# Rotary keys of a head pair: one whole split of the transposed bank, doubled tiles by GpSimd, and a low product over 64 rows

## The chip, the cores and the metric

The kernel runs on one core of one Trainium2 chip. The core's engines work side by side, each through its own queue of instructions: TensorE (PE in the profile, with PEld for its weight loads), VectorE (DVE), ScalarE (ACT), GpSimd (POOL) and SyncE (SP, which here issues most DMAs). Matmul results land in PSUM, in banks of 128 partitions by 512 fp32 values; everything else lies in SBUF, 128 partitions wide. GpSimd has no operation on PSUM in this kernel. The metric is device time of one execution in microseconds.

## What is computed

A trunk of two layers over 512 tokens of width 2048: a gated pooling mixer, then latent attention with 16 heads. The part that matters here is the score of a query with a key. A head's query and key have 128 plain channels and 64 rotary ones; the rotary key is the same for all heads but for the norm of the head's key.

```python
k = qk_norm_rope(concatenate([k_nope, k_rope]), k_norm_g, cos, sin)   # 128 + 64 channels
q = qk_norm_rope(q, q_norm_g, cos, sin)
for i in range(S // QBLOCK):                       # 4 blocks of 128 queries
    s = einsum('bqhd,bkhd->bhqk', q[:, q0:k_end], k[:, :k_end]) * scale
    s = where(mask, s, -1e30)                      # block-causal, chunks of 64
    p = softmax(s)
    outs.append(einsum('bhqk,bkhd->bqhd', p, v[:, :k_end]))
```

All of it is fp32.

## The kernel before

Every fp32 product is made of three products of a shorter type (float32r): a value x is split into a high part, x rounded to that type, and a low part, x minus the high part, and hi·hi + hi·lo + lo·hi are summed in PSUM. The split is a ScalarE copy (high) and a VectorE subtraction (low). `split` (line 153) does both, with the helper's line 154 in the profile for both of them.

The attention stage handles the 16 heads as eight head pairs. For each pair, key, value and query projections run in small pieces (lines 662 to 664 and 685 to 687 are their matmuls), and between them the scores, softmax and outputs of the pair before. Which piece comes when is written out by hand: a list of pieces with estimated times, and a main loop over 64 score units (pair, head, block of 128 queries) that fills the time between softmax steps with pieces. TensorE keeps exactly the order of the program; the instructions of the other engines are put in order by a planner.

Steps that the change and the prediction touch:

- `krot_unit` (line 713): GpSimd scales the rotary key by each head's norm into one tile, `krs`, two heads of 64 channels side by side.
- `tr_unit(hg, 2)` (lines 749 to 767): four TensorE transposes (line 754) bring `krs` to a PSUM bank, p: rows 0 to 63 are head 0's rotary channels, rows 64 to 127 head 1's, 512 tokens long. Then, for each head: GpSimd clears rows 64 to 127 of the low tile `kl` (762), ScalarE copies the head's 64 rows to the high tile `kh` twice, to its upper and lower half (763, 764), and VectorE writes the low part into the upper half of `kl` (765). From pair 1 on this unit stands in the main loop beside the sixth score unit of the pair before.
- `tr_unit(hg, 5)`: the same for the rotary query, whose high part goes to rows 0 to 63 and low part to rows 64 to 127 of one tile per head (781, 782). The other values of u transpose the plain channels of keys (0, 1) and queries (3, 4), all through line 776.
- `score_unit` (line 794): five matmuls (810) into one bank: three of the plain channels, one of the query tile (high over low) with `kh` (high twice), which gives hi·hi + lo·hi in a single product over 128 rows, and one of the same query tile with `kl` (low over zeros), which gives hi·lo, also over 128 rows.
- After it come the row maximum (813, 815), the exponential on ScalarE (823), the scaling on VectorE (829, 830), and the transposes of the probabilities (`pt_unit`, 838).

All these transposes share two PSUM banks of the tag "tr", which are used in turn: the next but one set of transposes waits until the set before has been read out. SBUF tiles of the tag "b" come from a pool of 32 buffers, also in turn.

Of the kernel before, what the change touches and what calls it, by code (L numbers as in the profile page):

```python
# [8 lines left out]
F32R = mybir.dt.float32r  # L9
I32 = mybir.dt.int32  # L10
AF = mybir.ActivationFunctionType
ALU = mybir.AluOpType
AX = mybir.AxisListType

P = 128
S = 512
# [31 lines left out]
def trunk_kernel(  # L48
# [17 lines left out]
    V, A, G, T = nc.vector, nc.scalar, nc.gpsimd, nc.tensor  # L66

    const = ctx.enter_context(tc.tile_pool(name="const", bufs=1))
    rpool = ctx.enter_context(tc.tile_pool(name="rpool", bufs=2))
# [3 lines left out]
    def xt(shape=(P, S), dt=F32):  # L73
        return xpool.tile(list(shape), dt, tag="x", name="xt")
# [4 lines left out]
    def at(dt=F32R, shape=(P, S)):  # L79
        return apool.tile(list(shape), dt, tag="a", name="at")  # L80

    def bt(shape=(P, S), dt=F32R):
        return bpool.tile(list(shape), dt, tag="b", name="bt")
# [10 lines left out]
    def sc():  # L94
        return ps.tile([P, S], F32, tag="sc", name="sc", bufs=2)

    def tr():
        return ps.tile([P, S], F32, tag="tr", name="tr", bufs=2)

    def f(ap):  # L100
        return ap.bitcast(F32)
# [51 lines left out]
    def split(src, hi, lo):  # L153
        return A.copy(hi, src), V.tensor_tensor(lo, src, f(hi), ALU.subtract)  # L154
# [112 lines left out]
    with ExitStack() as c1:  # L267
# [106 lines left out]
        with ExitStack() as c2:  # L374
            hp = c2.enter_context(tc.tile_pool(name="hp", bufs=2, **tile_))
            for j in range(NJ):
# [5 lines left out]
                hi = w7.tile([P, 4, 2, P], F32R, tag="hi", name="hi")  # L382
                lo = w7.tile([P, 4, 2, P], F32R, tag="lo", name="lo")
# [42 lines left out]
        for n, pair in enumerate((*range(18, 32), *range(16))):  # L426
# [7 lines left out]
            if n == 9:  # L434
                V.tensor_tensor(sq[0], sq[0], sq[1], ALU.add)
                p = ps7[0].tile([P, 2, H], F32, tag="k3", name="k3").rearrange("p h t -> p (h t)")
# [79 lines left out]
    for k in range(KD):  # L516
        hi, lo = at(), at()
        gsplit(xr[k], C_GKV + k, hi, lo)
        xkv.append((hi, lo))
        hi, lo = bt(), bt()  # L520
# [67 lines left out]
    kr = krb[:, 0:256].rearrange("p (t d) -> p t d", t=4)  # L588
# [48 lines left out]
    def small(n=8, tag="sm", bufs=6):  # L637
        return spool.tile([P, n], F32, tag=tag, name=tag, bufs=bufs)
# [107 lines left out]
    def tr_unit(hg, u):  # L746

        d = st[hg]
        if u == 2:

            d["kr"] = []
            p = tr()
            for t in range(4):
                T.transpose(p[:, t * P:(t + 1) * P], d["krs"][:, t * P:(t + 1) * P], ident)
            for h in range(2):
                src = p[h * 64:h * 64 + 64, :]
                if hg:
                    kh = bt()
                else:
                    kh = xt(dt=F32R) if h else rpool.tile([P, S], F32R, tag="r", name="kr0")  # L760
                kl = bt()
                G.memset(f(kl[64:128, :]), 0.0)
                A.copy(kh[0:64, :], src)
                A.copy(kh[64:128, :], src)
                V.tensor_tensor(kl[0:64, :], src, f(kh[0:64, :]), ALU.subtract)
                d["kr"].append((kh, kl))
            return
        p = tr()
        for t in range(4):
            if u < 2:  # L770
                src = d["kraw"][t // 2][:, t % 2, u * P:(u + 1) * P]
            elif u < 5:
                src = d["qraw"][t][:, u - 3, 0:128]
            else:
                src = d["qrot"][:, t * P:(t + 1) * P]
            T.transpose(p[:, t * P:(t + 1) * P], src, ident)  # L776
        if u == 5:
            q0, q1 = bt(), bt()
            for h, q in enumerate((q0, q1)):
                src = p[h * 64:h * 64 + 64, :]  # L780
                A.copy(q[0:64, :], src)
                V.tensor_tensor(q[64:128, :], src, f(q[0:64, :]), ALU.subtract)
            d["qr"] = (q0, q1)
            return
        ft = at if hg == 0 and u in (0, 3) else bt
        hi, lo = ft(), ft()
        if u in (3, 4):
            A.activation(hi, p, AF.Copy, scale=gqk)
            V.scalar_tensor_tensor(lo, p, gqk, f(hi), ALU.mult, ALU.subtract)
        else:  # L790
            split(p, hi, lo)
        d[("T", u)] = (hi, lo)

    def score_unit(hg, h, i):
        d = st[hg]
        n = (i + 1) * P
        if i == 2:

            gt = d[("G", h)] = bt(dt=F32)
            nc.sync.dma_start(gt, gates[2 * hg + h])  # L800
        s = sc()
        kh, kl = d[("T", h)]
        krh, krl = d["kr"][h]
        qh, ql_ = d[("T", 3 + h)]
        qr = d["qr"][h]
        qs = slice(i * P, (i + 1) * P)
        ops = [(qh[:, qs], kh[:, 0:n]), (qh[:, qs], kl[:, 0:n]), (ql_[:, qs], kh[:, 0:n]),
               (qr[:, qs], krh[:, 0:n]), (qr[:, qs], krl[:, 0:n])]
        for j, (l, r) in enumerate(ops):
            T.matmul(s[:, 0:n], l, r, start=(j == 0), stop=(j == 4))  # L810
        V.memset(s[0:64, n - 64:n], -1e30)
        nm = small(1, "nm", 4)
        V.tensor_reduce(nm, s[:, 0:n], AX.X, ALU.max)
        rq = d["rq"][:, 2 * i + h:2 * i + h + 1]
        V.scalar_tensor_tensor(nm, nm, -1.0, rq, ALU.mult, ALU.mult)
        d[("P", h, i)] = s, nm, rq
# [207 lines left out]
    for m, (key, w) in enumerate(keys):  # L1024
        n = last[keys[m - 4][0]] if m >= 4 else -1
# [48 lines left out]
    for m in range(len(seq) + 2):  # L1074
        now = seq[m] if m < len(seq) else None
        if now:
            hg, h, i = now
# [105 lines left out]
```

## Time and profile before

| | us |
|---|---|
| median of 3 runs | 1920.48 (1920.28 to 1922.47) |
| the profiled execution | 1920.45 |
| its span in the profile | 1918.7 |
| TensorE busy in the span | 1902.5 (99%) |
| VectorE busy | 1299.6 (68%) |
| ScalarE busy | 829.2 (43%) |
| GpSimd busy | 286.9 (15%) |

The profile shows one execution. A timeline row reads: start, duration, engine, line, operation, output tile <- input tiles, shape, how many in a row; in brackets how long the engine stood idle before it and what the profile takes for the releaser. In a row of a group, what follows the bar is the busy time, the mean of one in ns, and the idle time before. In a row of a line's instructions, three numbers in ns are the shortest, the median and the longest. Ends of matmuls are modelled, and one matmul overlaps the next, so how fast TensorE goes is read from the distance of their starts, not from their durations. Granted clock of TensorE was full (0.999) over the whole span.

The stage of the projection layers lasts until about 1450 us; the eight head pairs until about 1765 us, some 35.2 us each in the middle; the output projection takes the rest.

### The profile page before, as it was taken

The page shows a single profiled execution, that of the slowest core. Times are in us where ns is not written, and L with a number is a line of the kernel's source. Part 1 is how long each engine was busy: PE and PEld are TensorE (multiplying, and loading weights), DVE is VectorE, ACT ScalarE, POOL GpSimd, SP SyncE. Part 2 cuts the span into 40 slices and gives each one's busy share as a digit, 9 for nine tenths or more (in the row PEclk, how much of TensorE's full clock was granted, in tenths as well). Part 3 has the DMA queues.
Part 4 walks back from the last instruction along what each step waited for, and adds up shares of the span by engine and source line. Part 5 has one row for each costly group of instructions (what it writes and reads, how often), then busy time and mean ns, then how long its engine had stood idle before and what let it go on. Part 6 is the DMA issues. An engine that isn't in the chain of part 4 may idle for free.

```text
span 1918.7 us, 30196 instructions
## 1 busy us (share of the span) xinstructions
PE 1902.5 (99%) x11084; PEld 1688.6 (88%) x11084; DVE 1299.6 (68%) x2282; ACT 829.2 (43%) x1555; POOL 286.9 (15%) x436
## 2 busy tenths in 40 slices
PE   8999999999999999999999999999999999999999
PEld 7999999999999988888888888888888888988887
DVE  8677796897766786586695576574335888887332
ACT  8444433333333442332432354233236787775221
POOL 0433343333232100000000000000001332320000
PEclk9999999999999999999999999999999999999999
DMA  6555444444454556334334344334443232244642
GB/s 191 158 162 159 150 132 133 123 129 138 145 151 131 167 172 199 115 119 152 118 124 137 105 150 132 93 99 121 116 120 95 82 96 77 74 128 143 200 117 87
DMA packets 177077, 251.24 MB, mean 131 GB/s; under 512 B 15776, under 2 KB 96800, under 8 KB 176928
## 3 DMA queue, kind: packets, MB, share of 16 engines
q1 hardware_dynamic: 176640, 249.10, 42.3%
q8 instruction: 87, 1.43, 0.3%
q14 instruction: 62, 0.51, 0.1%
q10 hardware_dynamic: 288, 0.20, 0.0%
HBM read 216.21 MB, written 33.03 MB: 130 GB/s over the span
## 4 chain that ended last, share of the span: by engine, by line
PE 93%; DVE 3%; DMA 2%; ACT 1%; issue 1%; POOL 0%; SPq 0%; DVEq 0%; POOLq 0%; ACTq 0%
PE mm L149 16%; PE mm L151 16%; PE mm L150 16%; PE k L346 10%; PE k L344 9%; PE k L342 9%; PE k L339 3%; PE sc L810 2%; PE mm L662 1%; PE mm L664 1%; PE mm L663 1%; PE mm L685 1%; PE mm L686 1%; PE mm L687 1%; PE tr L838 1%; PE tr L776 1%
## 5 line engine op out<-in xcount | busy, mean ns | idle before, releaser
L131 ACT CAST whi<-raw 128x512 fp32r<-128x512 f32 (+2 forms) x424 | 256.2, 607 | 539.4 <-PE mm L150 439.9
L132 DVE TENSOR_TENSOR wlo<-raw,whi 128x512 fp32r<-128x512 f32 (+2 forms) x424 | 283.8, 670 | 242.7 <-ACT whi L131 239.7
L346 PE MATMUL k<-xc,lo 128*128 128x256 f32 x1680 | 417.4, 283 | 0.8 <-DVE lo L320 0.8
L344 PE MATMUL k<-xc,hi 128*128 128x256 f32 x1440 | 397.5, 283 | 0.0
L342 PE MATMUL k<-xc,hi 128*128 128x256 f32 x1440 | 396.8, 282 | 0.0
L151 PE MATMUL mm<-bt,wlo 128*128 128x512 f32 x944 | 368.0, 390 | 0.0
L149 PE MATMUL mm<-bt,whi 128*128 128x512 f32 x944 | 367.7, 390 | 0.0
L150 PE MATMUL mm<-bt,whi 128*128 128x512 f32 x944 | 367.0, 389 | 0.0
L320 DVE TENSOR_TENSOR lo<-raw,hi 128x1792 fp32r<-128x1792 f32 x120 | 249.3, 2078 | 131.7 <-ACT hi L319 131.5
L319 ACT CAST hi<-raw 128x1792 fp32r<-128x1792 f32 x120 | 203.2, 1693 | 285.7 <-PE k L346 172.5
L346 PEld LDWEIGHTS k<-xc,lo 128*128 128x128 f32 x1680 | 302.7, 190 | 8.3 <-DVE lo L320 2.0
L342 PEld LDWEIGHTS k<-xc,hi 128*128 128x128 f32 x1440 | 273.3, 190 | 5.0
L344 PEld LDWEIGHTS k<-xc,hi 128*128 128x128 f32 x1440 | 273.7, 190 | 0.0
L151 PEld LDWEIGHTS mm<-bt,wlo 128*128 128x128 f32 x944 | 177.1, 188 | 37.3 <-issue 0.5
L149 PEld LDWEIGHTS mm<-bt,whi 128*128 128x128 f32 x944 | 177.3, 188 | 36.9 <-ACT whi L131 0.2
L150 PEld LDWEIGHTS mm<-bt,whi 128*128 128x128 f32 x944 | 177.2, 188 | 36.7
L150 PE MATMUL mm<-at,whi 128*128 128x512 f32 x432 | 168.6, 390 | 0.3 <-DVE at L154 0.3
L149 PE MATMUL mm<-at,whi 128*128 128x512 f32 x432 | 168.8, 391 | 0.0
L151 PE MATMUL mm<-at,wlo 128*128 128x512 f32 x432 | 168.2, 389 | 0.0
L315 POOL TENSOR_TENSOR raw<-raw 128x256 f32<-128x256 f32 x120 | 97.5, 812 | 428.3 <-DVE raw L313 410.1
L316 POOL TENSOR_TENSOR raw<-raw 128x256 f32<-128x256 f32 x120 | 110.0, 917 | 9.2
L150 PEld LDWEIGHTS mm<-at,whi 128*128 128x128 f32 x432 | 81.1, 188 | 17.3 <-DVE at L154 0.6
(1137 smaller groups left out, 2714.2 us busy)
## 6 DMA issues: line engine op xcount, KB each, us to landing
raw<-awin SPq DMA_DIRECT2D x240, 256.0 KB, 3.4
raw<-awo SPq DMA_DIRECT2D x128, 256.0 KB, 2.7
raw<-bwin SPq DMA_DIRECT2D x80, 256.0 KB, 2.9
raw<-awg SPq DMA_DIRECT2D x64, 256.0 KB, 2.7
scr<-e SPq DMA_DIRECT2D x56, 256.0 KB, 2.7
raw<-bwo SPq DMA_DIRECT2D x56, 256.0 KB, 2.9
raw<-wkvb SPq DMA_DIRECT2D x32, 256.0 KB, 3.1
raw<-wqb SPq DMA_DIRECT2D x32, 192.0 KB, 2.4
```

Of the source, the lines that this page charges most:

```text
L131: wsplits[:] = (A.copy(hi[:, :n], raw[:, :n]).ins, V.tensor_tensor(lo[:, :n], raw[:, :n], f(hi[:, :n]), ALU.subtract).ins)
L132: V.tensor_tensor(lo[:, :n], raw[:, :n], f(hi[:, :n]), ALU.subtract).ins)
L149: T.matmul(dst, wh, xh, start=first, stop=False)
L150: T.matmul(dst, wh, xl, start=False, stop=False)
L151: T.matmul(dst, wl, xh, start=False, stop=last)
L315: G.tensor_tensor(c[:, :, 6, :], c[:, :, 4, :], c[:, :, 2, :], ALU.add)
L316: G.tensor_tensor(c[:, :, 7, :], c[:, :, 6, :], c[:, :, 3, :], ALU.add)
L319: A.copy(hi, c[:, :, 1:8, :])
L320: V.tensor_tensor(lo, c[:, :, 1:8, :], f(hi), ALU.subtract)
L342: T.matmul(dst, hi[:, j % 2, wi, :], xh[j][:, xi, :], start=first, stop=False, skip_group_check=True)
L344: T.matmul(dst, hi[:, j % 2, wi, :], xl[j][:, xi, :], start=False, stop=False, skip_group_check=True)
L346: T.matmul(dst, lo[:, j % 2, wi, :], xh[j][:, xi, :], start=False, stop=last, skip_group_check=True)
```

## The change

In `tr_unit(hg, 2)` the bank is split whole: one ScalarE copy of all 128 rows to `k0` and one VectorE subtraction of all 128 rows to a single low tile `kl`. `k0` then holds head 0's high rows above and head 1's below. GpSimd makes the doubled tiles from it: it copies `k0`'s lower half to both halves of `k1`, and then `k0`'s upper half over its lower half. The two clearings of low tiles are gone, and one low tile is needed instead of two.

The low tile now holds head 0's low rows in partitions 0 to 63 and head 1's in 64 to 127, with nothing to mask the other head. So the fifth matmul of a score unit contracts only the head's own 64 partitions, and the query's high part has to lie in the same partitions: for head 1 the query tile is turned over, low part above, high part below. The fourth matmul, over 128 rows with the doubled high tile, is indifferent to that.

```diff
@@ tr_unit, u == 2
-            d["kr"] = []
             p = tr()
             for t in range(4):
                 T.transpose(p[:, t * P:(t + 1) * P], d["krs"][:, t * P:(t + 1) * P], ident)
-            for h in range(2):
-                src = p[h * 64:h * 64 + 64, :]
-                if hg:
-                    kh = bt()
-                else:
-                    kh = xt(dt=F32R) if h else rpool.tile([P, S], F32R, tag="r", name="kr0")
-                kl = bt()
-                G.memset(f(kl[64:128, :]), 0.0)
-                A.copy(kh[0:64, :], src)
-                A.copy(kh[64:128, :], src)
-                V.tensor_tensor(kl[0:64, :], src, f(kh[0:64, :]), ALU.subtract)
-                d["kr"].append((kh, kl))
+            if hg:
+                k0, k1 = bt(), bt()
+            else:
+                k0, k1 = rpool.tile([P, S], F32R, tag="r", name="kr0"), xt(dt=F32R)
+            kl = bt()
+            split(p, k0, kl)
+            for half in (slice(0, 64), slice(64, 128)):
+                G.tensor_copy(k1[half, :], k0[64:128, :])
+            G.tensor_copy(k0[64:128, :], k0[0:64, :])
+            d["kr"] = (k0, kl[0:64, :]), (k1, kl[64:128, :])
             return
@@ tr_unit, u == 5
             for h, q in enumerate((q0, q1)):
                 src = p[h * 64:h * 64 + 64, :]
-                A.copy(q[0:64, :], src)
-                V.tensor_tensor(q[64:128, :], src, f(q[0:64, :]), ALU.subtract)
-            d["qr"] = (q0, q1)
+                hi, lo = q[h * 64:h * 64 + 64, :], q[64 - h * 64:128 - h * 64, :]
+                A.copy(hi, src)
+                V.tensor_tensor(lo, src, f(hi), ALU.subtract)
+            d["qr"] = (q0, q0[0:64, :]), (q1, q1[64:128, :])
             return
@@ score_unit
-        qr = d["qr"][h]
+        qr, qrh = d["qr"][h]
...
-               (qr[:, qs], krh[:, 0:n]), (qr[:, qs], krl[:, 0:n])]
+               (qr[:, qs], krh[:, 0:n]), (qrh[:, qs], krl[:, 0:n])]
```

## The prediction

> **What bounds the kernel now.** I read the top of the page first, then the chain that ended last, then the timeline of one head pair.
>
> ```profile
> PE 93%; DVE 3%; DMA 2%; ACT 1%; issue 1%; POOL 0%; SPq 0%; DVEq 0%; POOLq 0%; ACTq 0%
> ```
>
> TensorE carries 93% of the chain, so time can only be won where it stands still, and lost where it is given more work or a new wait. The change touches only the attention stage, where the scores run from 1480 to 1763 us, eight head pairs of about 35 us each. In that stage I looked for matmuls that start later than the one before them allows. A 512-column matmul is followed by the next after 0.227 us when nothing is late (the rows for this stand below, with the cost of small matmuls). In every middle pair one place is late. The timelines of ScalarE, VectorE and TensorE in one of them, just after the four transposes of the rotary k (start, duration, engine, line, in us):
>
> ```profile
> 1541.72 0.58 ACT L763 CAST bt<-tr 64x512 fp32r<-64x512 f32 x1 [0.86 <-PE tr L754]
> 1542.31 0.58 ACT L764 CAST bt<-tr 64x512 fp32r<-64x512 f32 x1
> 1542.92 0.56 ACT L823 ACTIVATE tt__15373<-sc,nm,qy 128x256 f32<-128x256 f32 x1
> ```
> ```profile
> 1542.92 0.68 DVE L765 TENSOR_TENSOR bt<-tr,bt 64x512 fp32r<-64x512 f32 x1 [0.56 <-ACT bt L764]
> ...
> 1544.31 0.34 DVE L830 TENSOR_SCALAR tt__15373<-tt__15373,sm 128x256 f32<-128x256 f32 x1
> ```
> ```profile
> 1544.27 0.40 PE L664 MATMUL mm<-wlo,at 128*128 128x512 f32 x1
> 1544.80 0.41 PE L838 MATMUL tr<-cs,tt__15373 128*128 128x128 f32 x2
> ```
>
> The exponential of a score row (L823) stands on ScalarE behind the two copies of the split, its scaling (L830) on VectorE behind the split's subtraction and a reduction that the engine takes in between, and the transposes of that row (L838) start only when the scaling is done: 1544.80 instead of 1544.27 + 0.23 = 1544.50. **0.30 us** lost. The next pairs repeat it, five in all; the last of them loses 1685.69 - 1685.15 - 0.23 = 0.31:
>
> ```profile
> 1685.15 0.40 PE L664 MATMUL mm<-wlo,at 128*128 128x512 f32 x1
> 1685.69 0.41 PE L838 MATMUL tr<-cs,tt__17629 128*128 128x128 f32 x2
> 1685.85 0.48 PE L662 MATMUL mm<-whi,at 128*128 128x512 f32 x1
> ```
>
> In the pair that is split first inside the loop, and in the last, the loss is larger and sits one step later:
>
> ```profile
> 1509.01 0.39 PE L664 MATMUL mm<-wlo,at 128*128 128x512 f32 x1
> ...
> 1509.67 0.69 DVE L765 TENSOR_TENSOR bt<-tr,bt 64x512 fp32r<-64x512 f32 x1
> ...
> 1510.51 0.63 PE L776 MATMUL tr<-cs,qt 128*128 128x128 f32 x4 [1.11 <-DVE qy L168]
> ```
> ```profile
> 1722.71 0.38 PE L838 MATMUL tr<-cs,tt__18213 128*128 128x128 f32 x2
> ...
> 1724.65 0.63 PE L776 MATMUL tr<-cs,qt 128*128 128x128 f32 x4 [1.56 <-DVE qy L168]
> ```
>
> The transposes of the q side (L776) need one of the two transposed banks, and the one whose turn it is still holds rotary k until the second head's subtraction (L765) ends, at 1510.36. The profile puts this wait down to a small VectorE operation that ends just after (line 168), on which these transposes do not depend; the same engine's subtraction before it is the one they need. Late by 1510.51 - 1509.01 - 0.23 = **1.27 us**, and in the last pair by 1724.65 - 1722.71 - 0.16 = **1.78 us** (0.16 for two transposes, as between 1685.69 and 1685.85). Together the rotary split costs TensorE 1.27 + 5 x 0.30 + 1.78 = **4.6 us**, which is the ceiling of what the change can win there.
>
> **The change part by part.**
>
> *The split of the bank.* Removed per pair: four ScalarE copies of 64 rows (0.58 each) and two subtractions (0.69 each); added: one copy and one subtraction of 128 rows, for which the same forms stand in the trace:
>
> ```profile
> L154 ACT CAST bt<-tr x15: 587/608/621, 1484.8 to 1736.5; 128x512 fp32r<-128x512 f32 x15
> L154 DVE TENSOR_TENSOR bt<-tr,bt x15: 665/691/693, 1485.5 to 1737.3; 128x512 fp32r<-128x512 f32 x15
> ```
>
> ScalarE gives back 4 x 0.58 - 0.61 = 1.7 us a pair, VectorE 0.69. The bank is free 0.61 + 0.69 after the copy starts instead of 3.8 us after. In the steady pair: copy 1541.72 to 1542.33, exponential until about 1543.0, scaling over by about 1543.7, before the 1544.50 at which its transposes are due, and still in time if one other VectorE operation of 0.6 us comes first. In the pair at 1509 the bank would be free near 1508.4 (needed 1509.24), in the last near 1722.5 (needed 1722.85), where the copy waits behind other ScalarE work until 1720.68 in the old order. What is late next there is nothing that I can see, so I count 4.2 of the 4.6 us as won and leave 0.4 for the last pair's thin margin and the contention below.
>
> *GpSimd's three copies.* No such copy is in the trace. Nearest rows:
>
> ```profile
> L762 POOL MEMSET bt<- 64x512 f32 x16 | 8.3, 521 | 0.9
> ```
> ```profile
> L720 POOL TENSOR_TENSOR tt__15238<-krr,sy 128x256 f32<-128x256 f32 x2 | 2.1, 1060 | 1.7 <-DVE nm L815 1.7
> ```
> ```profile
> 1551.57 0.67 PE L810 MATMUL sc<-bt 128*128 128x128 f32 x5
> ```
> ```profile
> 1528.44 0.50 POOL L741 TENSOR_TENSOR tt__15132<-qt,qcos 128x128 f32<-128x128 f32 x1 [22.09 <-ACT qt L691]
> ```
> ```profile
> L763 ACT CAST kr<-tr x1: 581/581/581, 1474.4 to 1474.4; 64x512 fp32r<-64x512 f32 x1
> ```
> ```profile
> 1481.11 0.27 PE L810 MATMUL sc<-kr,bt 128*128 128x128 f32 x1
> ```
>
> Lower end 0.52 each (same shape, nothing read), upper end 2 x 1.06 = 2.1 (two inputs, twice the columns); I take 0.7, nearer to the same shape. Three make 2.1 us, with ends 1.6 and 6.4 (rounded from 3 x 2.12); two memsets (1.04) go. They begin when ScalarE's copy is done, 1542.4, and the next pair's first score needs them at 1551.57: even the upper end leaves 2.8 us, so TensorE does not see them. Nothing is queued behind them: GpSimd's next work is 22 us away, as the row of its first operation in a pair shows. If that cover were gone, the price would be the copies themselves, 2 us a pair. In pair 0 the split's copy starts at 1474.4 and a score first reads the tile at 1481.1; 6.1 us are left for the copies, which covers 2.1 us nearly three times over, and the upper end but for 0.3. No DMA is added or moved, and no load is passed; the pool that held four tiles a pair holds three, so buffers come free no later.
>
> Against VectorE they are not free:
>
> ```profile
> 1503.92 0.86 DVE L132 TENSOR_TENSOR wlo<-raw,whi 128x512 fp32r<-128x512 f32 x1
> ```
> ```profile
> 1504.19 0.77 POOL L742 TENSOR_TENSOR tt__14569<-qt,qsin 128x64 f32<-128x64 f32 x1
> ```
>
> With a GpSimd operation beside it the subtraction took 0.86, where one of this shape otherwise takes 0.67 to 0.69 (L154 above). So each copy may hold VectorE by 0.2 to its own 0.7 us, right when the scaling is due. The slack of 0.8 us found above takes one such hold; two or three would bring back part of the 0.30.
>
> The Trainium skill, "SBUF — State Buffer", section "SBUF: two separate sides", calls the pair of ports that GpSimd and VectorE share an exclusive lock: whichever starts first keeps it for the whole instruction and the other blocks. By that rule a VectorE operation with two SBUF inputs would lose the full copy, so it speaks for the rival in which less of the stall goes; the rows above show a delay of 0.19 us beside a GpSimd time of 0.77, less than a full hold.
>
> *The low product over 64 rows.* Each of the 64 score units (8 pairs, 2 heads, 4 row blocks) now has a fifth matmul that contracts 64 rows, between matmuls over 128. The columns that stream are the same, so I give the matmul the same length. (The q side's four operations per pair keep their shapes and only change rows: nothing.) What is unknown is the price of going from the full array to half its rows and back. No such matmul is in the trace; the nearest in kind is the rotary latent, which switches between 128 and 64 columns of weights at every step:
>
> ```profile
> 1226.35 0.39 PE L579 MATMUL mm<-at,whi 128*128 128x512 f32 x1
> ...
> 1229.34 0.40 PE L579 MATMUL mm<-at,whi 128*128 128x512 f32 x1
> ```
> ```profile
> 1218.65 0.39 PE L151 MATMUL mm<-at,wlo 128*128 128x512 f32 x1
> ...
> 1221.82 0.39 PE L150 MATMUL mm<-at,whi 128*128 128x512 f32 x1
> ```
>
> 13 steps in 2.99 us are 0.230 each, against 14 in 3.17, 0.226 each, without switching: 4 ns a switch. The other end is the change from fp32 transposes to the split products:
>
> ```profile
> 1611.88 0.48 PE L662 MATMUL mm<-whi,at 128*128 128x512 f32 x1
> 1612.20 0.39 PE L663 MATMUL mm<-whi,at 128*128 128x512 f32 x1
> ```
>
> 0.32 us to the next instead of 0.23: 0.09 a switch. With two switches a unit and 64 units the ends are 128 x 0.004 = 0.5 us and 128 x 0.09 = 11.5 us. For a gain I find no row: half the weights' width saves none of the 0.23 above, so the lower end stays at 0.5. I take 0.5, the row that is a switch of the array's shape.
>
> **Sum.** -4.2 + 0.5 = -3.7 us on the profiled execution's 1920.45 us (the span below and 1.75 around it): 1916.75.
>
> ```profile
> span 1918.7 us, 30196 instructions
> ```
>
> The median of the runs shown is 1920.48, so the forecast is **1916.8 us**, 0.19% faster.
>
> **Rivals.**
>
> *Half the rows is a costly switch (slower).* Each of the 128 switches makes TensorE wait until the matmul before is through and its weights cannot be loaded ahead. Price 0.06 to 0.18 us a unit: 3.8 to 11.5 us, so 1920 to 1928. It cancels the gain at 4.2 / 64 = 0.066 us a unit and makes the kernel slower by 0.2% (3.8 us) from 0.126. Against it: 4 ns for the switch in columns. For it: rows and columns of the array need not behave alike, and 0.09 exists for another switch.
>
> The Trainium skill, "TensorEngine Tiling (Array Packing)", section "Tiling Modes", says that changing the tiling mode drains TensorE. By that rule this rival would hold; at the one change of mode that this trace has (128 to 64 columns) no drain of any size shows, 4 ns.
>
> *Less of the stall goes.* GpSimd's copies hold VectorE, or the new order on ScalarE and VectorE puts the reduction first: the five 0.30 stay, only 1.27 + 1.78 go. 1920.45 - 3.1 + 0.5 = 1917.9, up to 1920 if one large stall stays too. This is also the case in which the change does not do what it says.
>
> *More goes.* 1.7 us of ScalarE and 0.7 of VectorE a pair come free; one more place in the last pair where TensorE stands idle, 0.66, goes with it:
>
> ```profile
> 1703.99 0.41 PE L838 MATMUL tr<-cs,tt__17902 128*128 128x128 f32 x2 [0.66 <-DVE sc L811]
> ```
>
> 1920.45 - 4.6 - 0.7 + 0.5 = 1915.7, down to 1914 with other places of the kind.
>
> *A worse order.* ScalarE, VectorE and the load queue are ordered anew by a planner; a wait like that of the last pair (1.8 us) appears in one or several pairs: 1921 to 1926.
>
> **How the numbers follow.** Forecast 0.46, costly switch 0.22, less 0.14, more 0.12, worse order 0.06. A measurement of this kernel can tell about 0.2% from no change: under 1916.6 is faster, over 1924.3 slower. Faster: 0.25 of the forecast (its own range, 1915.5 to 1918.5, straddles the line) and all of "more": 0.37. Slower: 0.12 of the costly switch and 0.05 of the worse order: 0.17. Same: the rest of these cases and all of "less", 0.46. The range 1914.0 to 1923.5 leaves out the dear half of the costly switch, the worst orders, and little below.
>
> **What would show it.** Right: L776 follows without idle time in the pairs near 1510 and 1724; L838 comes 0.23 us after L664 in the middle pairs; each pair's period falls from 35.2 to 34.9; matmuls over 64 rows follow one another within 0.23 us at 512 columns; GpSimd's copies last 0.5 to 2.1 us and no matmul waits for them. Wrong: gaps of 0.06 us or more before and behind the matmul over 64 rows in all 64 units (costly switch); scalings on VectorE that stretch or start late beside a GpSimd copy (less); new idle time of TensorE at another line (order).

## The result, and the profile after

The changed kernel takes 1937.66 us (median of six runs, 1936.43 to 1938.31) against 1922.01 for the kernel before, measured beside it (six runs, 1920.28 to 1923.46): a ratio of 1.0082, with a 95% interval of 1.0069 to 1.0095. It is slower by about 16 us. The forecast was 1916.8, and its range ended at 1923.5. The execution that was profiled took 1937.78 us, against 1920.45 before. The top of the page of the kernel after:

```profile
span 1935.9 us, 30161 instructions
...
PE 1923.5 (99%) x11084; PEld 1691.5 (87%) x11084; DVE 1295.4 (67%) x2274; ACT 817.1 (42%) x1531; POOL 292.6 (15%) x444
...
PE 95%; DVE 2%; DMA 1%; ACT 1%; issue 1%; SPq 0%; POOL 0%; DVEq 0%; ACTq 0%; POOLq 0%
```

ScalarE and VectorE have less to do (829.2 and 1299.6 us before), TensorE as many instructions as before and 21 us more of "busy" time. Its share of the chain rose from 93 to 95%. So the loss is not, in the main, a new wait for another engine: TensorE itself has become slower, and the window of the attention stage says where (columns: stretch, its length, then busy time and count of PE, PEld, DVE, ACT, POOL; clock, DMA share, GB/s). First the kernel before, then the one after:

```profile
1456.00:1765.00 309.00, 304.04 (x1817) 271.63 (x1816) 257.93 (x839) 228.30 (x720) 76.08 (x160) 1.00 0.32 96
```
```profile
1456.00:1782.00 326.00, 324.74 (x1817) 274.58 (x1816) 253.73 (x830) 215.64 (x695) 83.66 (x168) 1.00 0.30 90
```

The same 1817 matmuls of the attention stage take 326.0 us instead of 309.0, at full clock: 17.0 us of the 17.2 by which the span has grown (1935.9 - 1918.7). Next, one score unit of 384 columns and the three matmuls behind it, in TensorE's timeline; before, then after. Ends are modelled, so the starts are what counts:

```profile
1612.66 1.05 PE L810 MATMUL sc<-bt 128*128 128x384 f32 x5
1613.55 0.39 PE L662 MATMUL mm<-whi,at 128*128 128x512 f32 x1
1613.78 0.40 PE L663 MATMUL mm<-whi,at 128*128 128x512 f32 x1
1614.02 0.40 PE L664 MATMUL mm<-wlo,at 128*128 128x512 f32 x1
```
```profile
1546.13 1.25 PE L808 MATMUL sc<-bt 128*128 128x384 f32 x5
1547.31 0.51 PE L662 MATMUL mm<-whi,at 128*128 128x512 f32 x1
1547.65 0.40 PE L663 MATMUL mm<-whi,at 128*128 128x512 f32 x1
1547.89 0.40 PE L664 MATMUL mm<-wlo,at 128*128 128x512 f32 x1
...
1548.58 0.39 PE L664 MATMUL mm<-wlo,at 128*128 128x512 f32 x1
1548.81 0.38 PE L836 MATMUL tr<-cs,tt__15365 128*128 128x128 f32 x2
```

From the first score matmul to the third matmul behind the unit it was 1.36 us and is 1.76: **0.40 us more in a unit**, with no wait shown. The last two rows are the place that lost 0.30 in every middle pair before: the transposes now follow L664 after 0.23, so that stall has gone, as forecast. The timeline of the weight loads (PEld) for the same two units shows what differs, before and then after:

```profile
1612.43 0.96 PEld L810 LDWEIGHTS sc<-bt 128*128 128x128 f32 x5
1613.38 0.19 PEld L662 LDWEIGHTS mm<-whi,at 128*128 128x128 f32 x1
```
```profile
1545.90 0.78 PEld L808 LDWEIGHTS sc<-bt 128*128 128x128 f32 x4
1546.94 0.18 PEld L808 LDWEIGHTS sc<-bt 64*128 64x128 f32 x1 [0.26 <-issue]
1547.31 0.19 PEld L662 LDWEIGHTS mm<-whi,at 128*128 128x128 f32 x1 [0.19 <-issue]
```

Before, the weights of the matmul behind a unit (L662) were loaded from 1613.38, 0.17 us ahead of its start at 1613.55. After, the load of the 64 rows waits 0.26 us, and the load behind it, which goes back to 128 rows, starts at 1547.31, the moment at which its matmul starts. Neither is loaded ahead any longer.

Taken over all 64 units, from the starts of the matmuls in both traces (medians in us, 16 units of each size; the order of the matmuls is the same in both):

| columns | before: fifth matmul behind the fourth, next, next but one | after | more in the unit, with one matmul further |
|---|---|---|---|
| 128 | 0.111, 0.112, 0.226 | 0.205, 0.254, 0.284 | 0.29 |
| 256 | 0.117, 0.118, 0.119 | 0.210, 0.314, 0.223 | 0.39 |
| 384 | 0.181, 0.174, 0.178 | 0.269, 0.370, 0.279 | 0.40 |
| 512 | 0.227, 0.231, 0.114 | 0.319, 0.424, 0.221 | 0.39 |

About 0.09 us is lost going in, 0.20 coming out (0.14 at 128 columns) and up to 0.1 at the matmul behind that, whatever the number of columns. From the 64-row matmul to the next it is 0.254, 0.314, 0.370 and 0.424 us: 0.057 for each 128 columns, the rate of a full stream (0.227 for 512), and 0.20 on top at every size. The 0.14 is the same 0.20, seen against a matmul of 128 columns that takes 0.112 before.

The 64 units together are 23.7 us longer, some 23 of it by the rows and 0.7 by a longer wait for a scaling in the last pair (the line from the list of waits below). Ten places at which TensorE stood idle before are 6.2 us shorter, and all else is 0.5 shorter: 23.7 - 6.2 - 0.5 = 17.0 us, the whole difference of the stage.

GpSimd's copies are as forecast (groups by line for the pairs 1 to 7: count, busy us and mean ns, idle time before):

```profile
L761 POOL CAST bt<-bt 64x512 fp32r<-64x512 f32 x14 | 8.7, 619 | 14.2 <-ACT bt L154 13.9
L762 POOL CAST bt<-bt 64x512 fp32r<-64x512 f32 x7 | 4.7, 673 | 0.4
```

and no matmul waits for them: TensorE's list of waits (us in total, times, longest) has only one of over 0.5 us in the attention stage, in the last pair.

```profile
PE tr L836 <- DVE tt__18347 L828: 1.0, 1, 1.0
```

### The profile page after: what moved, and what is told of

It is laid out like the page before. It is cut to its first block, busy times and chain, and to the rows that moved or that the text cites. A ratio compares the mean times of both kernels' runs of the same rounds, so it can differ in the third digit from the quotient of the medians.

```text
span 1935.9 us, 30161 instructions
## 1 busy us (share of the span) xinstructions
PE 1923.5 (99%) x11084; PEld 1691.5 (87%) x11084; DVE 1295.4 (67%) x2274; ACT 817.1 (42%) x1531; POOL 292.6 (15%) x444
## 4 chain that ended last, share of the span: by engine, by line
PE 95%; DVE 2%; DMA 1%; ACT 1%; issue 1%; SPq 0%; POOL 0%; DVEq 0%; ACTq 0%; POOLq 0%
PE mm L150 16%; PE mm L149 16%; PE mm L151 16%; PE k L346 10%; PE k L344 9%; PE k L342 8%; PE sc L808 3%; PE k L339 3%; PE mm L662 2%; PE mm L664 2%; PE mm L663 2%; PE mm L685 1%; PE mm L687 1%; PE mm L686 1%; PE tr L773 1%; PE tr L836 1%
```

## The experiments

The theory after this reading: a visit, that is a change from 128 rows to 64 and back, costs about 0.37 us, 23.7 us in all, and the split itself is worth the 4 to 6 us that its stalls took. Rivals: the loss belongs to the split and its GpSimd copies and not to the 64 rows; it is a price of each 64-row matmul and not of the visit; any change of the weights' shape costs it. Each run is compared with the kernel before on the same chip.

### The split without the 64 rows, and the 64 rows without the split

e1_full_rows keeps the whole split, but the low tile is doubled by GpSimd as well, and the fifth product goes over 128 rows. It then adds low times low of the rotary channels, which neither kernel has.

```diff
-            kl = bt()
-            split(p, k0, kl)
+            l0, l1 = bt(), bt()
+            split(p, k0, l0)
+            for x0, x1 in ((k0, k1), (l0, l1)):
+                for half in (slice(0, 64), slice(64, 128)):
+                    G.tensor_copy(x1[half, :], x0[64:128, :])
+                G.tensor_copy(x0[64:128, :], x0[0:64, :])
-            d["kr"] = (k0, kl[0:64, :]), (k1, kl[64:128, :])
+            d["kr"] = (k0, l0), (k1, l1)
...
-            d["qr"] = (q0, q0[0:64, :]), (q1, q1[64:128, :])
+            d["qr"] = (q0, q0), (q1, q1)
```

> The change with its low product put back on all 128 rows: GpSimd doubles the low tile as it doubles the high one (three more copies a pair), and the fifth matmul contracts the whole query tile with it, so that it adds lo*lo, a term that neither kernel computes. Theory (the price is the change of the array's rows, 0.37 us a score unit): the units go back to their old spacing and the late matmuls stay gone (5.5 us less than before in the traces), 1922.0 - 5.5 = 1916.5 us, between 1915 and 1919. Rival (the loss comes from the new order of ScalarE and VectorE or from GpSimd's copies beside VectorE): it stays near 1937, or goes above it with six copies.

Measured: 1919.97 us (11 runs) against 1920.84, ratio 0.9995 [0.9986, 1.0003]. The loss is gone, so the 64 rows carry it. The gain that was expected did not come either; that is taken up below.

e2_only_64 is the kernel before with one line changed:

```diff
-               (qr[:, qs], krh[:, 0:n]), (qr[:, qs], krl[:, 0:n])]
+               (qr[:, qs], krh[:, 0:n]), (qr[0:64, qs], krl[0:64, 0:n])]
```

> The kernel before with one edit: the fifth matmul of a score unit contracts rows 0 to 63 alone, of the same tiles. Theory (change of the array's rows): 64 units at 0.37 us, 1922.0 + 23.7 = 1945.7 us, and each 64-row matmul starts 0.09 us late and the one behind it 0.20 late, at all four column counts; the first 64 rows cost what the second do. Rival (split and GpSimd): 1922, no change.

Measured: 1938.6 us (4 runs) against 1920.84, ratio 1.0091 [1.0078, 1.0105]. The one line makes the whole loss. It is less than expected, and TensorE's timeline says why. The place in the middle pair that stalled for 0.30 us in the kernel before, in this kernel with the old split:

```profile
1549.75 0.40 PE L664 MATMUL mm<-wlo,at 128*128 128x512 f32 x1
1549.98 0.38 PE L838 MATMUL tr<-cs,tt__15373 128*128 128x128 f32 x2
```

0.23 us: the stall has gone although nothing was done about it. TensorE now comes 0.3 us later to the same place, and the scaling is ready. By the starts, the units are 22.6 us longer here and the old stalls 4.7 us shorter, among them all five of the middle pairs (0.30 each) and the one near 1510 (1.26). Of the 6.2 us that vanish in the changed kernel, 4.7 vanish without the split.

### A price per visit, or per matmul?

e3_two_halves is the changed kernel with the 64-row product cut into two of half the columns, one behind the other.

```diff
-        for j, (l, r) in enumerate(ops):
-            T.matmul(s[:, 0:n], l, r, start=(j == 0), stop=(j == 4))
+        for j, (l, r) in enumerate(ops[:4]):
+            T.matmul(s[:, 0:n], l, r, start=(j == 0), stop=False, skip_group_check=True)
+        for c in (0, n // 2):
+            T.matmul(s[:, c:c + n // 2], qrh[:, qs], krl[:, c:c + n // 2], start=False, stop=True,
+                     skip_group_check=True)
```

> The change with its 64-row product cut into two matmuls of half the columns each, one behind the other. If the price is paid per change of rows, the second one comes without it: two short matmuls instead of one cost some 0.11, 0.10, 0.07 and 0 us at the four column counts, 4.5 us in all, 1937.7 + 4.5 = 1942 us. If it is paid per 64-row matmul (its weights are never loaded ahead), the second pays 0.27 to 0.37 us in each of 64 units: 1955 to 1961 us.

Measured: 1940.18 us (4 runs) against 1920.84, ratio 1.0104 [1.0090, 1.0118]. That is 19.3 us above its kernel before, where the changed kernel is 15.7 above its own: 3.7 us for 64 more matmuls, near the 4.5 expected and far from the 17 or more of the rival. The price is paid for a visit, going in and coming out, not for each matmul.

### Rows, or any shape?

e12_half_columns is the kernel before with the fifth product for the first 64 queries of a block alone: its weights are 128 rows by 64 columns, at the same place in the unit. The product is left out for the other 64 queries.

```diff
-        for j, (l, r) in enumerate(ops):
-            T.matmul(s[:, 0:n], l, r, start=(j == 0), stop=(j == 4))
+        for j, (l, r) in enumerate(ops[:4]):
+            T.matmul(s[:, 0:n], l, r, start=(j == 0), stop=(j == 3))
+        T.matmul(s[0:64, 0:n], qr[:, i * P:i * P + 64], krl[:, 0:n], start=False, stop=True,
+                 skip_group_check=True)
```

> The kernel before, with the fifth product of a score unit over all 128 rows but over the first 64 queries of the block alone: its weights are 128 rows by 64 columns (the product of the high query with the low key is left out for the other 64 queries, in the rotary channels). Theory: what costs 0.37 us a unit is the change of the number of ROWS; a change of columns costs 4 ns, as the rotary latent's steps say, so 64 x 2 x 0.004 = 0.5 us more than before: 1921 to 1922. Rival: any change of the weights' shape between matmuls of one unit costs the same (the rotary latent is a case of its own): 64 x 0.37 = 23.7 less the 6 that hide, as with the 64-row product alone: about 1938.

Measured: 1921.56 us (10 runs) against 1921.06, ratio 1.0001 [0.9992, 1.0010]. In TensorE's timeline and that of its weight loads:

```profile
1612.83 0.88 PE L810 MATMUL sc<-bt 128*128 128x384 f32 x4
1613.54 0.34 PE L811 MATMUL sc<-bt 128*64 128x384 f32 x1
1613.72 0.40 PE L662 MATMUL mm<-whi,at 128*128 128x512 f32 x1
```
```profile
1613.37 0.14 PEld L811 LDWEIGHTS sc<-bt 128*64 128x64 f32 x1
1613.54 0.19 PEld L662 LDWEIGHTS mm<-whi,at 128*128 128x128 f32 x1
```

The 64-column load leads its matmul by 0.17 us, the next one its own by 0.18, and that matmul follows after 0.18 us, as behind a full one of 384 columns (0.174 in the table above). A change of columns costs nothing here. A change of rows costs 0.37.

### Where the gain of the split went

e4_zeroed_low clears the other half of each low tile on GpSimd instead of doubling, with one ScalarE copy and two 64-row subtractions, so that the fifth product goes over 128 rows and computes just what the kernel before does.

```diff
-            kl = bt()
-            split(p, k0, kl)
+            l0, l1 = bt(), bt()
+            G.memset(f(l0[64:128, :]), 0.0)
+            G.memset(f(l1[0:64, :]), 0.0)
+            A.copy(k0, p)
+            for h, l in enumerate((l0, l1)):
+                rows = slice(h * 64, h * 64 + 64)
+                V.tensor_tensor(l[rows, :], p[rows, :], f(k0[rows, :]), ALU.subtract)
```

> The change's whole copy and doubled high tiles, with two low tiles that GpSimd clears and VectorE fills by one subtraction of 64 rows for each head; the fifth matmul runs over 128 rows. The same result as before and after. Theory: 1916.5 to 1918 us, as the run with doubled low tiles, since the bank is free 0.61 + 2 x 0.69 us after the copy starts, still before the q side needs it. If the single subtraction is what frees the bank in time, the last pair's and the first pair's waits come back in part: 1918 to 1920.

Measured: 1920.61 us (11 runs) against 1920.84, ratio 0.9996 [0.9987, 1.0005]. The wait of 1.27 us near 1510 is gone, but of the last pair's only 0.7 us goes, 0.56 is lost near 1518, and the stall of the middle pairs is back, by another way. VectorE's timeline in that place:

```profile
1542.84 1.39 DVE L764 TENSOR_TENSOR bt<-tr,bt 64x512 fp32r<-64x512 f32 x2 [0.25 <-ACT bt L761]
...
1544.61 0.39 DVE L167 TENSOR_TENSOR qa<-qa,qv 128x8 f32<-128x8 f32 x1
```

Two subtractions of 64 rows take 1.39 us where one of 128 takes 0.69, and an operation on 8 columns (line 167) takes 0.39 instead of 0.15, beside a GpSimd copy. The scaling stands behind both, and the transposes (L841) lose 0.42 us in each middle pair instead of 0.31.

In e1_full_rows, whose 64 score units and other matmuls have the same order as before, the starts can be compared one by one. It wins at ten places: 0.43, 1.27, five times 0.31, 0.82, 1.73 and 0.39, together 6.2 us. It loses 6.1 us at others, above all 0.27, 0.14 and 0.42 in middle pairs, then 0.74, 0.23 and 0.16 from 1710 to 1714, and one large wait behind the first score unit of the last pair. TensorE's timeline there:

```profile
1722.86 1.30 PE L809 MATMUL sc<-bt 128*128 128x512 f32 x5
...
1728.22 0.67 PE L809 MATMUL sc<-bt 128*128 128x128 f32 x5
1731.04 0.63 PE L837 MATMUL tr<-cs,tt__18379 128*128 128x128 f32 x4 [2.14 <-DVE tt__18379 L829]
...
1731.89 0.63 PE L150 MATMUL mm<-at,whi 128*128 128x512 f32 x1
1732.32 0.63 PE L151 MATMUL mm<-at,wlo 128*128 128x512 f32 x1
...
1734.88 0.43 PE L151 MATMUL mm<-at,wlo 128*128 128x512 f32 x1
```

The transposes wait 2.14 us for the scaling of the scores of 1722.86, which are complete before 1724.2. VectorE's timeline shows what stood between:

```profile
1724.19 0.68 DVE L154 TENSOR_TENSOR at<-at 128x512 fp32r<-128x512 f32 x1
1724.79 0.74 DVE L788 SCALAR_TENSOR_TENSOR bt<-tr,gqk,bt 128x512 fp32r<-128x512 f32 x1
1725.45 0.68 DVE L154 TENSOR_TENSOR at<-at 128x512 fp32r<-128x512 f32 x1
...
1726.16 0.67 DVE L132 TENSOR_TENSOR wlo<-raw,whi 128x512 fp32r<-128x512 f32 x1
1726.86 0.69 DVE L781 TENSOR_TENSOR bt<-tr,bt 64x512 fp32r<-64x512 f32 x1
1727.58 0.69 DVE L812 TENSOR_REDUCE nm<-sc 128x1 f32<-128x512 f32 x1
...
1730.40 0.49 DVE L829 TENSOR_SCALAR tt__18379<-tt__18379,sm 128x512 f32<-128x512 f32 x1
```

The reduction of the row maximum starts 3.4 us after the scores are there, behind five splits, and the scaling another 2.8 later. This is the stretch in which the splits of the output projection's weights (lines 131, 132) and of its inputs (line 154) come on top. The windows of the same run say how full VectorE is (third pair of numbers):

```profile
1710.00:1720.00 10.00, 9.23 (x56) 7.95 (x57) 9.94 (x33) 8.50 (x29) 4.45 (x9) 1.00 0.50 140
1725.00:1731.00 6.00, 3.89 (x23) 3.19 (x21) 5.85 (x14) 3.98 (x10) 0.00 (x0) 1.00 0.63 192
1731.50:1734.90 3.40, 3.40 (x11) 2.63 (x10) 2.88 (x9) 1.20 (x4) 0.00 (x0) 0.51 0.55 181
```

9.94 us of 10, and 5.85 of 6. In these pairs TensorE waits for VectorE, and where the kernel before waited for the bank (1.78 us) this one waits for the scaling. The last row adds a surprise: after this wait the granted clock is about half (0.51) for 3.4 us. Eight matmuls start 0.427 us apart (1731.89 to 1734.88) instead of 0.229, which with the step before them is another 1.5 us. The Trainium skill, "TensorE: Matmul & The Clock Gate", section "Part 1: The HAM clock gate (the "warmup" mystery)", gives 426.7 ns from start to start at 512 columns for its half clock; the rows above agree (1732.32 - 1731.89 = 0.43).

### Attempts to keep the gain

If VectorE's load in the last pairs is the cause, moving the scaling to ScalarE should keep the gain. e5_scale_act does so in the last pair, and e6_before_scale is the kernel before with the same edit.

```diff
-        st["scale"] = V.tensor_scalar(pe[:, 0:n], pe[:, 0:n], sm, None, ALU.mult)
+        if hg == nhg - 1:
+            st["scale"] = A.activation(pe[:, 0:n], pe[:, 0:n], AF.Copy, scale=sm)
+        else:
+            st["scale"] = V.tensor_scalar(pe[:, 0:n], pe[:, 0:n], sm, None, ALU.mult)
```

> The run on all rows with doubled low tiles, and in the last head pair the scaling of the probabilities done by ScalarE instead of VectorE. Theory (what the split wins is given back in the last pair, where VectorE is busy without a break from 1710 to 1731 us, and TensorE, which now arrives 3.6 us earlier, waits for it and then runs at half clock for some 4 us): some 1.5 us leave VectorE ahead of that place, the wait of 2.1 us shrinks below 1 and the 1.6 us of slow clock go: 1920.0 - 3 = 1917 us, between 1915.5 and 1918.5. Rival (the loss there is the planner's order, not VectorE's load): 1920, no change.

> The kernel before with the same move of the last pair's scaling to ScalarE, and nothing else. Theory: in the kernel before the last pair waits first for the transposed bank (1.7 us), which ScalarE's and VectorE's old split still holds, so little is won: 1919 to 1920.8. If the last pair's VectorE load were worth the 3 us by itself, without the split, it would give 1918.

Measured, against 1920.67: e5 1919.71, ratio 0.9994 [0.9985, 1.0002]; e6 1920.29, ratio 0.9999 [0.9990, 1.0007]. Neither can be told from no change. The edit was at the wrong units: the scores that are late belong to the seventh pair, since the last pair's own follow behind that stretch, and in e5 the wait stays at 2.12 us. What differs in e5's trace is the clock: it stays full behind that wait, and by the starts the attention stage is 1.7 us shorter than before the change, where e1's is 0.1 shorter. e9_scale_pair6 moves the scaling of the seventh pair (`hg == nhg - 2`).

> The run on all rows with doubled low tiles, and ScalarE does the scaling for the scores of the seventh of the eight pairs, the units that run while the eighth pair is prepared, from 1694 to 1731 us. The earlier run with this move changed the eighth pair's own units, which lie behind the stretch in question, so it could not test it. Theory (VectorE, busy without a break from 1710 to 1731, gives the split's gain back there): about 2 us leave it, the wait of 2.1 us at the last transposes shrinks below 1: 1920.0 - 1.5 = 1918.5 us, or 1917 with the slow clock gone. Rival (it is the order of the work, or ScalarE behind it): 1919.5 to 1920.5.

Measured: 1921.31 against 1921.13, ratio 1.0002 [0.9993, 1.0011]. The largest of TensorE's waits in e9's attention stage:

```profile
PE tr L840 <- ACT tt__18379 L830: 2.9, 1, 2.9
```

The wait has grown from 2.1 to 2.9 us and now names ScalarE, where the scaling queues behind splits as it did on VectorE. Of the plain form of the theory, "take the scaling off VectorE", nothing is left.

e7_last_old keeps the old split in the last pair alone, with no GpSimd copies there; e8_old_scale is e7 with the edit of e5, and e10_old6_scale e7 with that of e9.

```diff
+            if hg == nhg - 1:
...
+                    own, other = slice(h * 64, h * 64 + 64), slice(64 - h * 64, 128 - h * 64)
+                    G.memset(f(kl[other, :]), 0.0)
+                    A.copy(kh[own, :], src)
+                    A.copy(kh[other, :], src)
+                    V.tensor_tensor(kl[own, :], src, f(kh[own, :]), ALU.subtract)
+                    d["kr"].append((kh, kl))
+                return
             if hg:
                 k0, k1 = bt(), bt()
```

> The run on all rows with doubled low tiles in pairs 0 to 6; the last pair's split as in the kernel before (four ScalarE copies and two subtractions of 64 rows, two clearings by GpSimd, no GpSimd copies). In the trace with the copies four small VectorE operations beside them take 0.57 to 0.59 instead of 0.16 us, 1.7 us in all, in the stretch where VectorE has no idle time. Theory (GpSimd's copies hold VectorE there): VectorE gets 1.7 back and pays 0.69 for the second subtraction, but the bank is held longer again and its wait of up to 1.7 us returns: 1918 to 1920. Rival (the copies cost nothing, the single subtraction is what counts): slower by 0.7 us or more, 1920.7 or above.

> Both edits of the last pair together: old split without GpSimd copies, scaling by ScalarE; pairs 0 to 6 with the whole split and 128-row products. Theory: 1916 to 1918 us, the middle pairs' gain kept. Rival: the last pair is limited by something else, 1920.

> The run with the eighth pair's split as before and no GpSimd copies in it, and the seventh pair's scaling on ScalarE. Theory: the wait for the transposed bank there (1.7 us in the run without the move) shrinks by what leaves VectorE, up to 1 us: 1918.2 us. Rival: ScalarE, with four copies and the scaling, becomes late itself: 1919.3 or above.

Measured: e7 1919.25 and e8 1918.62 against 1920.67, ratios 0.9991 [0.9982, 1.0000] and 0.9991 [0.9982, 0.9999]; e10 1921.2 against 1921.13, ratio 0.9994 [0.9985, 1.0003]. In e7 and e8 the wait for the scaling shrinks to 0.2 us and the old one for the bank returns, about the same size as before the change:

```profile
PE tr L786 <- DVE bt L763: 1.7, 1, 1.7
```

e10 went as its rival said: the wait for the bank is 2.3 us, and transposes wait 1.1 and 0.7 us for scalings on ScalarE. e8 is the fastest version found, some 0.09% below the kernel before (about 1.7 us). That is less than the 0.2% that the forecast took as told apart, and it is the best of several tries, with an interval that ends just short of no change.

Last, e11_gpsimd_sub is e1 with part of VectorE's work given to GpSimd: the low parts of nine of the output projection's weight tiles.

```diff
-                      V.tensor_tensor(lo[:, :n], raw[:, :n], f(hi[:, :n]), ALU.subtract).ins)
+                      (sub or V).tensor_tensor(lo[:, :n], raw[:, :n], f(hi[:, :n]), ALU.subtract).ins)
...
-            parts[key] = load_w(*w)
+            parts[key] = load_w(*w, sub=G if key[0] is out_part and key[2] < 8 else None)
```

> The version with the whole split and 128-row fifth products (doubled high and low tiles by GpSimd, low times low added), and GpSimd instead of VectorE does the low part's subtraction of the output projection's early weights, some of which fall into the last pairs, where VectorE is busy 99% of the time. Theory: VectorE's load in the last pair is what makes the scaling late after the first score unit of the 8th pair: the wait of 2.1 us near 1731 shrinks and the time falls to about 1918.0 to 1918.7. Rival: the wait follows from GpSimd's operations holding VectorE and from the order on the two queues, not from the amount of work: it stays, 1920 or above, with more small VectorE operations stretched beside GpSimd.

Measured: 1920.4 against 1921.06, ratio 0.9996 [0.9987, 1.0005]. Its rows of windows and of TensorE's timeline:

```profile
1710.00:1720.00 10.00, 8.81 (x55) 7.35 (x54) 8.85 (x25) 8.97 (x29) 7.87 (x15) 1.00 0.29 75
```
```profile
1731.25 0.33 PE L809 MATMUL sc<-bt 128*128 128x128 f32 x1 [0.44 <-POOL bt L763]
1732.31 0.63 PE L837 MATMUL tr<-cs,tt__18379 128*128 128x128 f32 x4 [0.73 <-DVE tt__18379 L829]
```

VectorE is at 8.85 of 10 instead of 9.94, and the wait for the scaling falls from 2.14 to 0.73 us. That speaks for its load as a cause of the wait; the planner's order changes with the edit too, and no run tells the two apart. The clock stays full. But other things are late now: a score waits 0.44 us for a tile that GpSimd doubles, the query's transposes 0.44 and a set of probabilities' transposes 0.43 near 1722, where e1 had none. By the starts the attention stage is only 0.3 us shorter than e1's, though the wait is 1.4 us shorter and the slow clock (1.5) is gone: most of what was won at one place was lost at others within 20 us.

## Why the prediction was wrong, step by step

- **What bounds the kernel: right.** TensorE's chain decides, and each us of it was seen in the time.
- **"The low product over 64 rows ... I take 0.5": this is the step that failed, and it decides the sign.** Two switches a unit were priced at 4 ns each from the latent's change of columns, "the row that is a switch of the array's shape". They cost 0.37 us a unit, some 23 us in 64. The extrapolation was from columns to rows: e12 shows that the 4 ns was right for columns at this very place, e2 that the change of rows alone makes the loss. The upper end, 0.09 a switch and 11.5 us in all, was half of what came; it had been taken from the change of fp32 transposes to split products, with only the delay of the switch itself, while here the matmul behind and the one after it are late too.
- **The rival "half the rows is a costly switch"** described what happened, down to the weights that are not loaded ahead, with 0.06 to 0.18 us a unit; the size was two to six times that (0.37). The rule of the Trainium skill, "TensorEngine Tiling (Array Packing)", section "Tiling Modes", that a change of tiling mode drains TensorE, stood beside it. The trace of after agrees with it for rows (0.37 us a visit) and e12 does not for columns (nothing to be seen), if a matmul with 64 columns of weights is such a change, which no run here tells. The trace of before had columns alone and could not test the rule for rows. So the 4 ns was no evidence against this rival, though the prediction counted it as such.
- **"I count 4.2 of the 4.6 us as won": the stalls went, the time did not.** In the changed kernel ten idle places lost 6.2 us, among them all that were forecast (1.27, five times 0.31, 1.73) and the 0.66 of "more goes" (0.82 by the starts). But 4.7 us of these go in e2 as well, where the split is the old one: a slower TensorE simply reaches the places later. And where TensorE is not slowed (e1), the same 6.2 us are won and 6.1 lost again.
- **"What is late next there is nothing that I can see": the second step that failed.** Next, in e1, is the softmax of the last pairs, with VectorE busy 99% of the stretch from 1710 to 1720. That load stood in the trace of before, as the row of its windows below says (9.57 of 10); the prediction shows VectorE's order in one middle pair, and for the last pair only TensorE's rows. The rival "a worse order", a wait like the last pair's 1.8 us, is what e1 shows, 2.14.
- **ScalarE and VectorE give back 1.7 and 0.69 us a pair: right to within a quarter.** Their busy time fell by 829.2 - 817.1 = 12.1 and 1299.6 - 1295.4 = 4.2 us, against 13.6 and 5.5 for eight pairs.
- **GpSimd's copies at 0.7 us, hidden: right** in the changed kernel (0.62 and 0.67; no matmul waits for them). That they hold VectorE was right, and in e1 the hold is a full one. The prediction read less from the subtraction at 1503.92 that took 0.86, because it put beside it GpSimd's operation of 1504.19. The rows below fit the operation before that one: it ends at 1504.23, and from there the subtraction takes 0.55 more. The operation of 1504.19 looks held itself: it took 0.77, where the next one of its shape took 0.31. In e1, with six copies a pair, VectorE operations on 8 columns took up to 0.59 instead of 0.16: of the 40 that start during a copy none ends before the copy does, and 24 end 0.015 to 0.024 us after it, as the one of 1719.62. Where VectorE began first, the copy was late: beside the subtraction of 1722.13, which took 0.68 as always, a copy took 1.03. (The one exception found, at 1509.28 in the changed kernel, starts 0.004 us after its copy.)

The window of the kernel before in the last pairs, and GpSimd's rows around the subtraction of 1503.92:

```profile
1710.00:1720.00 10.00, 9.74 (x63) 8.74 (x62) 9.57 (x31) 9.04 (x33) 7.35 (x15) 1.00 0.38 113
```
```profile
1503.77 0.46 POOL L741 TENSOR_TENSOR tt__14568<-qt,qcos 128x128 f32<-128x128 f32 x1 [1.58 <-ACT qt L691]
...
1504.92 0.31 POOL L743 TENSOR_TENSOR tt__14569<-qt,qsin 128x64 f32<-128x64 f32 x1
```

The holds in e1, in VectorE's timeline and GpSimd's:

```profile
1719.62 0.57 DVE L166 TENSOR_TENSOR qa<-qy 128x8 f32<-128x8 f32 x1
...
1722.13 0.68 DVE L132 TENSOR_TENSOR wlo<-raw,whi 128x512 fp32r<-128x512 f32 x1
```
```profile
1719.47 0.70 POOL L762 CAST bt<-bt 64x512 fp32r<-64x512 f32 x1 [3.02 <-issue]
...
1722.25 1.03 POOL L763 CAST bt<-bt 64x512 fp32r<-64x512 f32 x1
```

Put together: forecast -4.2 + 0.5; in the run 23.7 for the units with 64 rows, 6.2 off for the idle places and 0.5 off for small changes elsewhere, 17.0 us in all.

What stays open: why a change of rows stops the loading ahead (the traces show that it does, not by what means), whether 32 rows or another place in the unit costs the same, which wasn't tried, and which order of the splits in the last two pairs would keep the 6 us. e9 and e11 moved work between engines, and the waits moved with it.

## What to carry to other kernels

Half the contraction rows save nothing in a stream of full matmuls, and each visit to them costs about 0.37 us here: pad with zeros or with a doubled operand, or gather such products so that many share one visit (in e3 two in one visit cost 3.7 us more over 64 units, not another 17 to 24). Price an unknown operation by rows that differ from it in the same dimension; where there are none, the bound is open above, and a cheap experiment (one line, e2) settles it. Before counting a stall as won, look at the whole stretch behind it, the last iterations above all: an engine that is nearly full there (96% in the kernel before) may be what is late next.

## What was unexpected in the hardware

- Going from 128 to 64 rows and back costs 0.09 us in, 0.14 to 0.20 out and up to 0.1 more, for either half of the rows and at 128, 256, 384 and 512 columns; going from 128 to 64 columns and back costs nothing that can be seen (e12).
- After a wait of 2.14 us in e1 TensorE ran at half its clock for 3.4 us (0.51 granted from 1731.5 to 1734.9). After one of 2.12 us at the same place in e5's trace the clock stayed full. So such a wait can cost another 1.5 us, and does not always. The Trainium skill, "TensorE: Matmul & The Clock Gate", section "Part 1: The HAM clock gate (the "warmup" mystery)", has an activity window of some 3.4 us whose phase the program does not set; that would allow both, but an idle time of 2.14 us is shorter than that window.
- The mean granted clock of each execution is below 1.000 in 30 of 44 executions of e1, e5, e9 and e10, whose longest wait there is 2.1 to 2.9 us, in 3 of 10 of e12 (2.3), in 4 of 11 of e6 and 19 of 96 of the kernel before (1.6), and in none of 33 of e7, e8 and e11 (1.7 at most). In e5 the five executions at 1.000 took 1918.1 to 1919.0 us and the six below it 1919.7 to 1922.5. So the clock is a likely part of what the attempts lost. It is not shown, since the mean doesn't say where in an execution the clock fell.
- A GpSimd copy of 64x512 stretches an 8-column VectorE operation with two inputs from 0.16 to as much as 0.59 us, until the copy is through (40 of 40 in e1). A subtraction of 512 columns that began 0.12 us before a copy took its usual 0.68, and the copy 1.03 instead of 0.61 to 0.70.
